# Neighbourhood attention on one core: keys in strips of eight columns with one value tile per row group, and nine of twelve second-stage units by seven products

## The chip, the cores and the metric

The kernel runs on one core of a Trainium2 chip. The metric is the device time of one execution in microseconds; the median of the runs is given. TensorE (PE) multiplies matrices, VectorE (DVE), ScalarE (ACT) and GpSimd (POOL) work element by element, and SyncE (SP) issues nearly all DMA transfers, in the order of its program.

## The reference, cut to what matters

One layer: an RMS norm, a projection of 2048 tokens of 1024 numbers onto queries, keys, values and a gate (4 x 1024 columns), neighbourhood attention on a grid of 32 rows by 64 columns with 16 heads of 64, a gate, an output projection, a residual and a final RMS norm.

```python
def reference(x, norm_0, w_in_0, rpb_0, w_out_0, norm_1, w_in_1, w_out_1, norm_f):
    h = rmsnorm(x, norm_0)
    q, k, v, gate = jnp.split(h @ w_in_0, 4, axis=-1)
    o = neighbourhood_attention(q, k, v, rpb_0)   # 16 heads of 64
    x = x + (o * jax.nn.silu(gate)) @ w_out_0
    return rmsnorm(x, norm_f)
```

Each token attends to 8 rows by 16 columns of keys around it, clipped at the grid's edges, with a bias that depends on the head and on the two offsets:

```python
rs = jnp.clip(r - kh // 2, 0, rows - kh)
...
s = jnp.where(col_valid[None, None], s + bias[None], NEG_INF)
p = jax.nn.softmax(s.reshape(B, H, nb, NA_QBLOCK, kh * NA_KBLOCK), axis=-1)
...
o = jnp.einsum('bhnqkj,bknjhd->bnqhd', p, vr)
```

## The kernel before

**Precision.** The projections split each float32 operand into a high and a low part and multiply three times (high by high, high by low, low by high). One tile of 128 by 512 results over 1024 inputs so costs 24 matmuls of 512 columns. Scores are done the same way; transposes and value products are float32.

**Stage one** (`stage_one`, line 546) works on the first 1024 tokens: all values, then the twelve units (kind, j) of k, q and g with j from 0 to 3, 256 columns each. A unit is a 2 by 2 block product, done by `seven_products` (line 378) in seven products of 12 matmuls, 84, where four plain tiles take 96. It costs sums and splits on DVE and ACT (`form`, `sum_`, `add`, `out_`, lines 390 to 431); `evac` and `give` (lines 309 and 321) evacuate results, split k into two parts, put q into query order, apply the gate's function, and store to DRAM.

**Stage two** (`stage_two`, line 756) does the second 1024 tokens: all values, and by seven products only the units of `units_two` (line 221). The remaining units stand in `halves` (line 222) and are done later in the plain way by `projections` and `group` (lines 868 and 346), 24 matmuls for each tile.

**The attention loop** (lines 1337 to 1356) has 64 turns and two more to drain. There are 32 pieces of work, the head pairs p = 0 to 7 by the row groups T = 0 to 3 of eight query rows (`order`, line 893), and each takes two turns, for column groups C = 0, 1 and then 2, 3 of 16 columns. So one tile of queries is 8 rows by 16 columns, 128 tokens. `KEY_ROWS` and `KEY_COLS` give the keys it can see: 11, 15, 15 or 12 rows by 24, 32, 32 or 24 columns.

In turn i the program emits, in this order: loads and biases (`begin`), matmuls from the filling (`feed`), the normalisation of turn i - 1, the transposes of turn i - 2 (`turns`), the scores of turn i, and the value products of turn i - 2 (`values`). Every engine works in program order. A score tile goes from PSUM through DVE, which adds the bias and takes the maximum (line 995), ACT's exponential with its sum (line 998), DVE's reciprocal (line 1004), POOL's scaling (line 1006), TensorE's transposes (line 1011), and copies to SBUF by DVE for the first half of the queries (line 1036) and by ACT for the second (line 1035, and the rest after it), to the value products (line 1056). POOL also makes the biases (`bias`, line 970): six sums whenever the head pair or the kind of row group changes.

**The filling.** `feed(n)` draws n matmuls from the projections that are left and then from the output projection (`outputs`), which needs all head pairs of a row group. `amount` (line 1272) says how many for each turn: 22 in each of the first 48 turns and 19.67 in the last 18. Up to 12 may be drawn ahead when an evacuation was just emitted (line 1280). The program's clock counts filling matmuls; stores and loads are put off by so many of them (`store`, `later_loads`, `due`), and `begin` emits all loads that are still put off.

**Values.** `evac_v` stores values to DRAM by head pair; `copy_v` (line 942), called throughout both stages, copies the 24 or 32 columns that each column group sees from DRAM to DRAM into `vc`, four rows interleaved on a partition index; `load_v` (line 932) loads one such tile for each piece and column group. `blocks` (line 61) cuts the keys of a row group into blocks of four rows: two that both halves of the queries (four rows each) see, and one or two that one half sees. The last block of row groups 0, 1 and 2 has three rows and so a copy of its own on ACT.

## Time and profile before

| | us |
|---|---|
| median of 3 runs | 1085.62 (1084.97 to 1085.65) |
| the profiled execution | 1086.36 |
| its span, first to last instruction | 1084.5 |

In the profile's lines a row names the line of the kernel, the engine, the operation, the tiles (out<-in), shapes and a count; after the bar come the busy time in us, the mean of one in ns, and the engine's idle time just before with what ended it. In the order of time a row begins with the start and the length in us. PE stands for TensorE's matmuls, PEld for its weight loads. The granted clock is that of TensorE as a share of full speed. Ends of matmuls are modelled, so counts of matmuls in a stretch are better than their busy time.

The seven products of stage one run from 96.6 to 325 us, the values of stage two to 414 us, its seven products to 471 us, the attention loop with its filling to about 1028 us, and the last output rows to the end.

### The profile page before, as it was taken

Reading aid. Unit: us, or ns where it says so; the run is one execution under the profiler, and the core shown is the slowest. Engines: PE = TensorE matmul, PEld = TensorE weight load, DVE = VectorE, ACT = ScalarE, POOL = GpSimd, SP = SyncE. Lnnn points to the kernel's source line nnn. Section 1 sums busy time; section 2 is a strip of 40 time slices with the busy share of each in tenths; the row PEclk is TensorE's granted clock in tenths of the full one; section 3 lists DMA queues with packets and bytes.
Section 4 is the critical chain, followed back from the end, with each engine's and each line's share of the span. In section 5 each row is a group of like instructions: output and inputs, shape, how many; then the busy total and the mean of one; then the engine's idle time right before and its main releaser. Section 6 shows DMA issues by size and latency. Waiting matters only on the chain.

```text
span 1084.5 us, 21929 instructions
## 1 busy us (share of the span) xinstructions
PE 1071.1 (99%) x7657; PEld 877.1 (81%) x7657; DVE 703.2 (65%) x1644; ACT 531.2 (49%) x1345; POOL 357.9 (33%) x474
## 2 busy tenths in 40 slices
PE   9999999999999999999999999999999999999997
PEld 6888888888888888887888888888888787888885
DVE  5376778778997535576555555664676786776643
ACT  7545334333434334346555555564576565665431
POOL 0000222312221000017545534444447656566200
PEclk9999999999999999999999999999999999999999
DMA  9633557574764366889868876886899787887442
GB/s 313 212 97 106 202 173 210 163 232 146 256 188 143 108 172 170 258 277 310 245 205 267 253 216 204 255 269 200 246 319 294 230 268 231 274 262 226 126 149 78
DMA packets 145901, 231.90 MB, mean 214 GB/s; under 512 B 13824, under 2 KB 61184, under 8 KB 145792
## 3 DMA queue, kind: packets, MB, share of 16 engines
q1 hardware_dynamic: 145648, 230.25, 68.2%
q8 instruction: 61, 1.00, 0.4%
q14 instruction: 48, 0.39, 0.1%
q10 hardware_dynamic: 144, 0.26, 0.1%
HBM read 171.73 MB, written 73.40 MB: 226 GB/s over the span
## 4 chain that ended last, share of the span: by engine, by line
PE 92%; DVE 3%; DMA 1%; ACT 1%; issue 1%; SPq 0%; POOL 0%; ACTq 0%; DVEq 0%; POOLq 0%
PE pp L411 23%; PE pv L531 16%; PE o L1056 8%; PE s L988 6%; PE pp L359 6%; PE pp L357 6%; PE pp L355 6%; PE po L1254 6%; PE po L1252 5%; PE po L1250 5%; PE ph L1011 5%; PE zp L1269 1%; DMA k_hi<-hi 1%; DMA land<-in_xt_dram 0%; DVE f L394 0%
## 5 line engine op out<-in xcount | busy, mean ns | idle before, releaser
L1006 POOL TENSOR_SCALAR x<-x,st 128x360 f32<-128x360 f32 (+5 forms) x256 | 143.0, 578 | 235.0 <-DVE st L1004 192.3
L970 POOL TENSOR_TENSOR em<-e,mk 128x480 f32<-128x480 f32 (+5 forms) x160 | 136.3, 886 | 138.3 <-DMA raw<-in_xt_dram 135.0
L998 ACT ACTIVATE x<-x,st 128x360 f32<-128x360 f32 (+5 forms) x256 | 151.8, 595 | 44.4 <-DVE st L995 44.4
L411 PE MATMUL pp<-h,f 128*128 128x512 f32 x480 | 155.4, 389 | 0.0
L430 POOL TENSOR_TENSOR tmp<-tmp,rb 128x512 f32<-128x512 f32 x36 | 58.9, 1637 | 270.6 <-DVE tmp L428 223.7
L411 PE MATMUL pp<-t,f 128*128 128x512 f32 x540 | 130.0, 390 | 0.3 <-DVE u L422 0.2
L995 DVE CUSTOM_DVE_ANT_0 x<-s,em 128x360 f32<-128x360 f32 (+5 forms) x256 | 124.0, 539 | 5.3 <-PE s L988 1.4
L411 PEld LDWEIGHTS pp<-t,f 128*128 128x128 f32 x540 | 101.2, 188 | 22.2 <-DVE u L422 1.2
L359 PE MATMUL pp<-h,w 128*128 128x512 f32 x288 | 115.1, 400 | 0.0
L357 PE MATMUL pp<-l,w 128*128 128x512 f32 x288 | 113.2, 393 | 0.0
L355 PE MATMUL pp<-h,w 128*128 128x512 f32 x288 | 113.1, 393 | 0.0
L1035 ACT ACTIVATE pta<-ph 96x256 f32<-96x256 f32 (+1 forms) x224 | 58.5, 333 | 104.3 <-PE ph L1011 104.3
L1036 DVE COPY pta<-ph 128x384 f32<-128x384 f32 (+3 forms) x128 | 60.7, 514 | 72.7 <-PE ph L1011 72.5
L411 PEld LDWEIGHTS pp<-h,f 128*128 128x128 f32 x480 | 90.1, 188 | 18.8
L1254 PE MATMUL po<-wol,gh 128*128 128x512 f32 x252 | 100.3, 398 | 0.0
L1252 PE MATMUL po<-woh,gl 128*128 128x512 f32 x252 | 98.9, 393 | 0.0
L1250 PE MATMUL po<-woh,gh 128*128 128x512 f32 x252 | 98.9, 392 | 0.0
L1056 PEld LDWEIGHTS o<-pta,vt 96*64 96x64 f32 (+2 forms) x1792 | 83.6, 137 | 17.2 <-issue 10.2
L1056 PE MATMUL o<-pta,vt 96*64 96x128 f32 (+4 forms) x1792 | 92.3, 254 | 1.4 <-DVE pta L1036 1.0
L411 PE MATMUL pp<-l,f 128*128 128x512 f32 x240 | 93.4, 389 | 0.0
L531 PE MATMUL pv<-wh,h 128*128 128x512 f32 x256 | 88.1, 390 | 0.0
L531 PE MATMUL pv<-wh,l 128*128 128x512 f32 x256 | 88.0, 389 | 0.0
(148 smaller groups left out, 1916.6 us busy)
## 6 DMA issues: line engine op xcount, KB each, us to landing
raw<-in_wg_dram SPq DMA_DIRECT2D x126, 256.0 KB, 5.1
e<-in_rpb_dram SPq DMA_DIRECT2D x54, 240.0 KB, 3.9
vt<-vc SPq DMA_DIRECT2D x64, 192.0 KB, 3.7
row<-in_xr_dram SPq DMA_DIRECT2D x32, 256.0 KB, 4.3
vd<-v SPq DMA_DIRECT2D x32, 256.0 KB, 3.0
k_hi<-hi SPq DMA_DIRECT2D x32, 256.0 KB, 2.6
k_lo<-lo SPq DMA_DIRECT2D x32, 256.0 KB, 3.8
vc<-vd SPq DMA_DIRECT2D x32, 256.0 KB, 4.4
```

The lines of the kernel that those rows point to most:

```text
L355: nc.tensor.matmul(p, wh[w, b][:, cols], hh[k, c], start=(k == 0), stop=False)
L357: nc.tensor.matmul(p, wh[w, b][:, cols], hl[k, c], start=False, stop=False)
L359: nc.tensor.matmul(p, wl[w, b][:, cols], hh[k, c], start=False, stop=(k == NK - 1))
L411: nc.tensor.matmul(B[n, P], t[:, int(m == 2), c], x[k][int(m == 1)], start=P in (1, 6, 5) and k == 0 and m == 0, stop=k == 3 and m == 2, s ...
L531: nc.tensor.matmul(ps[t], a[:, o], b, start=k == 0 and m == 0, stop=k == NK - 1 and m == 2)
L970: (nc.gpsimd if attending[0] or not s else nc.vector).tensor_tensor(sh(t), E[p, s][:, u0 + 4:u1 + 4, v0 + 8:v1 + 8], sh(MK[0][:, m0:m0 + n ...
L998: nc.scalar.activation(X[i, C][s], X[i, C][s], AF.Exp, bias=st[:, s:s + 1], scale=-1.0, accum_out=st[:, 2 + s:3 + s])
L1006: nc.gpsimd.tensor_scalar(X[i, C][s], X[i, C][s], st[:, 4 + s:5 + s], 0.5, op0=OP.mult, op1=OP.mult)
L1056: nc.tensor.matmul(o[s * 64:s * 64 + 64, C * 128 + q0:C * 128 + q0 + nq], vt[C][:k, g - g0_, s * 64:s * 64 + 64], t[:k, at:at + nq], start ...
L1250: nc.tensor.matmul(p, gh, woh[q, j], start=(i == 0), stop=False)
L1252: nc.tensor.matmul(p, gl, woh[q, j], start=False, stop=False)
L1254: nc.tensor.matmul(p, gh, wol[q, j], start=False, stop=(i == NK - 1))
```

## The change

The tokens of a grid row are put in the order (column within a strip, strip), with eight strips of eight columns; `x` for the norm's rows and the transposed `x` come to the chip in that order. Values are stored in token order, and one load per piece brings all eight strips: partition = (key row, column within the strip), 4 KB on each. Keys are put back into column order when they are split; queries, gate and output into the order (strip, row, column). The query tile is the same 8 by 16 tokens, with its halves now by columns, so `strips` takes the place of `blocks`: blocks are strips of eight columns by all 11, 15, 15 or 12 rows, 88, 120, 120 or 96 keys. Score tiles, masks and biases are laid out strip by strip. The copies `vc` from DRAM to DRAM go.

Apart from this, `units_two` has nine units in place of three, and the filling of the first 48 turns falls to 9.5 matmuls a turn, with 8 more in each of the first three; the amount that may be drawn ahead falls from 12 to half of a turn's amount.

```diff
-def blocks(T):
-    r0, r1 = KEY_ROWS[T]
+def strips(C):
     out = []
-    for g in range(r0 // 4, (r1 + 3) // 4):
-        halves = [h for h in range(2) if abs(2 * T + h - g) <= 1]
-        out.append((g, 4 * g - r0, min(4, r1 - 4 * g), halves[0] * 64, len(halves) * 64))
+    for s in range(KEY_COLS[C][0] // 8, KEY_COLS[C][1] // 8):
+        halves = [h for h in range(2) if abs(2 * C + h - s) <= 1]
+        out.append((s, s - KEY_COLS[C][0] // 8, halves[0] * 64, len(halves) * 64))
...
-    units_two = [(k, j) for j in range(1) for k in "kqg"]
-    halves = [(k, j, 1, c) for j in range(1, 4) for g in (("k", "q", "g") if j < 3 else ("k", "qg")) for c in (2, 3) for k in g]
+    units_two = [(k, j) for j in range(3) for k in "kqg"]
+    halves = [(k, j, 1, c) for j in range(3, 4) for g in ("k", "qg") for c in (2, 3) for k in g]
...
     def tiled(t):
-        return t.rearrange("p (r C c) -> p C r c", r=8, c=16)
+        return t.rearrange("p (r c s) -> p s r c", c=8, s=8)
 
     def blocked(t):
-        return t.rearrange("p (C r c) -> p C r c", r=8, c=16)
+        return t.rearrange("p (s r c) -> p s r c", r=8, c=8)
+
+    def by_place(t):
+        return t.rearrange("p (r c s) -> p r s c", c=8, s=8)
+
+    def by_column(t):
+        return t.rearrange("p (r s c) -> p r s c", s=8, c=8)
...
-        nc.scalar.activation(hi, t, AF.Copy)
-        nc.vector.tensor_tensor(lo, t, hi.bitcast(F32), OP.subtract)
+        nc.scalar.activation(by_column(hi), by_place(t), AF.Copy)
+        nc.vector.tensor_tensor(by_column(lo), by_place(t), by_column(hi.bitcast(F32)), OP.subtract)
...
-    def load_v(p, T, C):
+    def load_v(p, T):
         r0, r1 = KEY_ROWS[T]
-        g0_, g1_ = r0 // 4, (r1 + 3) // 4
-        c0, c1 = KEY_COLS[C]
-        def block():
-            VT[p, T, C] = t = vp([128, 4, 128], F32, "vt")
-            nc.sync.dma_start(t[:4 * (c1 - c0), :g1_ - g0_], vc[p, C][:, g0_:g1_])
-
-        return [block]
-
-    def copy_v(p, C, h):
-        must(*[("v", p // 4, t) for t in range(8 * h, 8 * h + 8)])
-        c0, c1 = KEY_COLS[C]
-        g = slice(512 * h, 512 * h + 512)
-        nc.sync.dma_start(vc[p, C].rearrange("(r c) g d -> c r (g d)", r=4)[:, :, g],
-                          vd[p // 4][p % 4].rearrange("r c g d -> c r (g d)")[c0:c1, :, g])
+        must(*[("v", p // 4, t) for t in range(r0 // 2, (r1 + 1) // 2)])
+        rows = vd[p // 4][p % 4].rearrange("(k s) d -> k s d", s=8)[8 * r0:8 * r1]
+        VT[p, T] = t = vp([128, 1024], F32, "vt").rearrange("p (s d) -> p s d", s=8)
+        nc.sync.dma_start(t[:8 * (r1 - r0)], rows)
...
-        sh = lambda a: a.rearrange("p (u v) -> p u v", v=v1 - v0)
+        sh = lambda a: a.rearrange("p (s u v) -> p s u v", u=u1 - u0, v=8)
...
-                sh(t), E[p, s][:, u0 + 4:u1 + 4, v0 + 8:v1 + 8], sh(MK[0][:, m0:m0 + n]), OP.add)
+                sh(t), E[p, s][:, u0 + 4:u1 + 4, v0 + 8:v1 + 8].rearrange("p u (s v) -> p s u v", v=8), sh(MK[0][:, m0:m0 + n]), OP.add)
...
-                    nc.tensor.matmul(pst[s], qq[a, qs], kk[a, :r1 - r0, c0:c1], start=(m == 0), stop=(m == 2))
+                    nc.tensor.matmul(pst[s], qq[a, qs], kk[a, :r1 - r0, c0:c1].rearrange("p r (s c) -> p s r c", c=8), start=(m == 0), stop=(m == 2))
...
             for h in range(2):
-                four = sum(b[2] == 4 for b in halves_[h])
-                k = 4 * width(C)
+                n = len(halves_[h])
                 put = (lambda o, i_: nc.scalar.activation(o, i_, AF.Copy)) if h else nc.vector.tensor_copy
-                put(slots[:k, h, :2 * four], ph[h][:k, :128 * four].rearrange("p (n q) -> p n q", q=64))
-                if four < len(halves_[h]):
-                    k = halves_[h][four][2] * width(C)
-                    put(slots[:k, h, 2 * four:2 * four + 2],
-                        ph[h][:k, 128 * four:128 * four + 128].rearrange("p (n q) -> p n q", q=64))
+                put(slots[:k, h, :2 * n], ph[h][:k, :128 * n].rearrange("p (n q) -> p n q", q=64))
...
     early = 96 * (12 - len(units_two)) + 192
-    amount = [early / 48] * 48 + [(384 - 30) / 18] * 18
+    first = 8
+    amount = [(early - 3 * first) / 48] * 48 + [(384 - 30) / 18] * 18
+    calm_debt = amount[0] / 2
+    for i in range(3):
+        amount[i] += first
...
-        while credit[0] > 0 or credit[0] > -12 and clock[0] - state["event"] < calm:
+        while credit[0] > 0 or credit[0] > -calm_debt and clock[0] - state["event"] < calm:
...
-        if 0 < i <= N:
-            p, T, cs = pairs[i - 1]
-            later_loads(load_v(p, T, cs[0]) + load_v(p, T, cs[1]), 0, 2)
+        if i % 2 == 0 and i < N:
+            load_v(*order[m])
```

More of the change, by code (lines that the diff above doesn't have):

```diff
@@ L1006, in normalise, with split @@
                 nc.gpsimd.tensor_scalar(X[i, C][s], X[i, C][s], st[:, 4 + s:5 + s], 0.5, op0=OP.mult, op1=OP.mult)
-    def turn(dst, i, C, s, blk, q0, nq):
-        g, lr, nr = blk[:3]
-        w = width(C)
-        nc.tensor.transpose(dst[:nr * w], X[i, C][s][q0:q0 + nq, lr * w:(lr + nr) * w],
-                            ident[q0:q0 + nq, q0:q0 + nq])
-    def split(T):
-        bl = blocks(T)
-        return [b for b in bl if b[4] == 128], [b for b in bl if b[4] == 64]
+    def split(C):
+        return [b for b in strips(C) if b[3] == 128], [b for b in strips(C) if b[3] == 64]
     def turns(i):
         p, T, cs = pairs[i]
-        full, part = split(T)
-        halves_ = [full + [b for b in part if b[3] == 64 * h] for h in range(2)]
+        k = 8 * (KEY_ROWS[T][1] - KEY_ROWS[T][0])
         for C in cs:
+            full, part = split(C)
+            halves_ = [full + [b for b in part if b[2] == 64 * h] for h in range(2)]
             t = PT[i, C] = pa([128, 768], F32, "pta")
```

69 lines of the change are left out of this document (32 added, 37 removed).

## The prediction

> **What bounds the kernel now.** I read the page first, then the table of stretches, then the order of time inside one turn of the attention loop.
>
> ```profile
> span 1084.5 us, 21929 instructions
> ...
> PE 1071.1 (99%) x7657; PEld 877.1 (81%) x7657; DVE 703.2 (65%) x1644; ACT 531.2 (49%) x1345; POOL 357.9 (33%) x474
> ...
> PE 92%; DVE 3%; DMA 1%; ACT 1%; issue 1%; SPq 0%; POOL 0%; ACTq 0%; DVEq 0%; POOLq 0%
> ```
>
> TensorE is busy for 99% of the span and carries 92% of the chain that ended last. Matmul ends are modelled, so busy time is not work; the work is read from counts per stretch. The next fence has the stretches of all engines (busy time and count of each engine, granted clock, DMA share, GB/s), and then the same stretches for line 995 alone, which runs eight times in a turn of the loop.
>
> ```profile
> core 0: us, PE busy (x) PEld busy (x) DVE busy (x) ACT busy (x) POOL busy (x), PEclk, DMA share, GB/s
> 300.00:400.00 100.00, 100.00 (x443) 82.77 (x442) 64.07 (x93) 37.66 (x68) 9.87 (x6) 1.00 0.53 153
> ...
> 499.40:614.90 115.50, 115.50 (x1084) 94.75 (x1078) 62.01 (x206) 64.33 (x202) 61.10 (x100) 1.00 0.80 251
> 614.90:784.60 169.70, 169.70 (x1734) 139.51 (x1733) 95.75 (x276) 94.38 (x276) 74.56 (x108) 1.00 0.75 233
> 784.60:889.20 104.60, 104.04 (x1075) 84.42 (x1072) 78.74 (x217) 66.76 (x194) 64.50 (x86) 1.00 0.88 278
> ...
> 499.40:614.90 115.50, 24.02 (x112) 1.00 0.80 251
> 614.90:784.60 169.70, 40.92 (x152) 1.00 0.75 233
> 784.60:889.20 104.60, 25.83 (x96) 1.00 0.88 278
> ```
>
> From 300 to 400 us, 443 matmuls of 512 columns ran in 100 us: 0.226 us each, at full granted clock. In the three attention stretches there are 112/8 = 14, 152/8 = 19 and 96/8 = 12 turns, so a turn lasts 8.25, 8.93 and 8.72 us. No other engine is near its limit now: the fullest are DVE with 78.74/104.60 = 75% in the third stretch and POOL with 62%.
>
> One turn in order of time, row group 0:
>
> ```profile
> 523.74 0.73 PE L1011 MATMUL ph<-ident,x 64*96 64x64 f32 x17
> 525.10 0.43 DVE L995 CUSTOM_DVE_ANT_0 x<-s,em 128x264 f32<-128x264 f32 x1
> 527.08 0.39 PE L355 MATMUL pp<-h,w 128*128 128x512 f32 x1
> 527.15 0.57 ACT L998 ACTIVATE x<-x,st 128x352 f32<-128x352 f32 x1
> 528.25 0.62 ACT L495 ACTIVATE qh<-qr 128x512 fp32r<-128x512 f32 x1
> 528.99 0.68 DVE L496 SCALAR_TENSOR_TENSOR ql<-qr,qh 128x512 fp32r<-128x512 f32 x1
> 531.18 0.39 PE L355 MATMUL pp<-h,w 128*128 128x512 f32 x1
> 531.78 0.22 DVE L1004 RECIPROCAL st<-st 128x2 f32<-128x2 f32 x2
> 531.95 0.74 PE L1011 MATMUL ph<-ident,x 64*128 64x64 f32 x17
> 532.13 2.03 POOL L1006 TENSOR_SCALAR x<-x,st 128x264 f32<-128x264 f32 x4 [9.66 <-DVE st L1004]
> 532.45 0.75 DVE L1036 COPY pta<-ph 128x256 f32<-128x256 f32 x2 [0.45 <-PE ph L1011]
> 534.11 4.71 POOL L970 TENSOR_TENSOR em<-e,mk 128x264 f32<-128x264 f32 x6
> ```
>
> The turn runs from transposes to transposes, 523.74 to 531.95. Line 355 is every third filling matmul; from 527.08 to 531.18 there are six triples, 18 matmuls in 4.10 us, 0.2278 each. A turn has 22 of them, 5.01 of its 8.21 us; 3.2 us are scores, transposes and value products. DVE and ACT finish in the shadow of the filling. So the filling is TensorE work and also the cover for everybody else's latency.
>
> **The change part by part.** *Matmuls.* Six units (k, q, g for j = 1 and 2) leave the loop's filling, where each takes 96 matmuls on the second half of the tokens, and join the second stage with seven products of 12, or 84. Removed: 576 x 0.2278 = 131.2 us. Added: 504 x 0.226 = 113.9 us. On TensorE this is -17.3 us. The counts of scores, transposes and value products are the same: column strips give 2 whole and 1 or 2 half blocks as row blocks did.
>
> *Thinner turns.* Filling falls from 22 to 9.5 per turn in the first 48 turns (17.5 in the first three). That is 12.5 x 0.2278 = 2.85 us less cover: by TensorE alone the three stretches go from 8.25, 8.93 and 8.72 to 5.40, 6.08 and 5.87 us a turn. What is late next is the loop that goes through DVE and ACT in their program order: line 995, exponentials, the filling's evacuations and splits, reciprocal, the copies of line 1036, line 995 again. In row group 0 it is 525.10 to 527.72 for line 995 and exponentials (2.62 us), 0.62 + 0.68 for splitting q in every other turn, 0.22, and 0.75: 4.9 us. The 9.5 fillings bring about 0.8 further ACT operations of 0.62 us, 0.5: 5.4 with the q split, 4.8 to 4.9 without it, against TensorE's 5.40. For 15 key rows the same rows are longer:
>
> ```profile
> 651.22 1.02 DVE L1036 COPY pta<-ph 128x384 f32<-128x384 f32 x2 [0.35 <-PE ph L1011]
> 652.39 0.66 DVE L995 CUSTOM_DVE_ANT_0 x<-s,em 128x480 f32<-128x480 f32 x1
> 655.04 0.58 ACT L998 ACTIVATE x<-x,st 128x360 f32<-128x360 f32 x1
> ```
>
> 652.39 to 655.62 is 3.23; with 1.30, 0.22, 1.02 and 0.5 the loop is 6.3 us with a q split and 5.7 without, against 6.08 and 5.87. I take waits of 0 in row group 0, 0.1 x 19 = 1.9 in the second stretch and, since the output evacuations fall there, 0.3 x 12 = 3.6 in the third: +5.5 us. The ends are 0 (all hidden, as now) and 0.5 in each of 45 turns, 22 us.
>
> *The first turns.* The pipeline starts behind a DVE backlog:
>
> ```profile
> 483.47 0.43 DVE L995 CUSTOM_DVE_ANT_0 x<-s,em 128x264 f32<-128x264 f32 x1
> 491.48 5.15 POOL L970 TENSOR_TENSOR em<-e,mk 128x264 f32<-128x264 f32 x6
> 496.62 2.02 POOL L1006 TENSOR_SCALAR x<-x,st 128x352 f32<-128x352 f32 x4
> 498.92 0.74 PE L1011 MATMUL ph<-ident,x 64*128 64x64 f32 x17
> ```
>
> The second pair's transposes (498.92) come 0.3 us behind its normalisation, which stands behind six bias sums, so this moment is set by POOL and DVE, not by filling. Up to it TensorE now has 4 x 22 = 88 fillings, then 3 x 17.5 + 9.5 = 62. The 26 missing ones, 5.9 us, are idle time if nothing else moves; with less filling in DVE's queue (one operation of 0.69 us) I take +5. Ends: 0 and 6.
>
> *Layout.* Keys in strips make the moving operand of the scores runs of 8 elements in place of 24 or 32. Mean times of such a matmul:
>
> ```profile
> L988 PE MATMUL s<-kt,qh 64*128 64x360 f32 x128 | 18.0, 346 | 0.0
> L988 PE MATMUL s<-kt,qh 64*128 64x352 f32 x64 | 11.1, 350 | 0.9 <-DVE lo L342 0.9
> ```
>
> 15 runs of 24 take no longer than 11 runs of 32, so I take 0. The upper end is 1 ns for each further run, about 33 x 6 pairs x 64 turns = 13 us. Tokens ordered with the strip innermost make q's evacuations, k's splits and the gate product read every eighth element. No row shows that. The nearest contiguous rows and the fullest DVE stretch (the last three units of the first stage):
>
> ```profile
> L428 DVE TENSOR_TENSOR tmp<-pp,u 128x512 f32<-128x512 f32 x30 | 20.6, 688 | 19.8 <-PE pp L411 19.3 <-issue 0.5
> L342 DVE TENSOR_TENSOR lo<-tmp,hi 128x512 fp32r<-128x512 f32 x19 | 12.9, 681 | 3.2 <-ACT hi L341 3.2
> ...
> sum 57.21, PE 57.00 PEld 46.86 DVE 54.20 ACT 23.12 POOL 15.31; mean PE 19.00 PEld 15.62 DVE 18.07 ACT 7.71 POOL 5.10
> ```
>
> At no extra cost the price is 0; at twice the time, 8 operations more of 0.69 us in those units make DVE 59.7 of 57.2 us: 2.5 us. Elsewhere DVE has room. I take +1. The Trainium skill, page "SBUF — State Buffer" (section on the port formula, its note on cachelines), speaks against this edit: a line is 16 bytes, and full rate wants two accesses in each; a step of 32 bytes gets one. By it the term would be the 2.5 us end, and nothing else in the sum would move; no row here can show it.
>
> *Copies and loads.* The 64 copies of values from DRAM to DRAM go, and one load of 4 KB rows takes the place of four. On the chain that ended last DMA has 1%, so this is 0, at DMA shares of 0.75 to 0.88. Of ACT's copies of transposes 96 (three row groups, 32 each) merge into their neighbours:
>
> ```profile
> L1035 ACT ACTIVATE pta<-ph 96x128 f32<-96x128 f32 x48 | 13.0, 271 | 0.0
> ```
>
> The two forms of 48 take 26 us in 48 turns, 0.54 a turn; about half returns as wider copies. It is off the loop above, where line 1036 is as long: 0, at best 0.1 us a turn.
>
> **Sum.** Against the profiled execution's own time, 1086.36 us (span 1084.5 and 1.9 around it): -17.3 + 5.5 + 5 + 1 = -5.8, 1080.6. The median of the runs stands 0.74 lower: 1079.8, so **1080**.
>
> **Rivals.** *All is covered.* The waits are 0, the start costs 0: 1085.6 - 17.3 = 1068.3. For it: slack of all engines in the table. Against: the start rows. Chance 0.2.
>
> *The loop eats it.* Waits of 0.25 us in each of 45 turns in place of 5.5 in all, and the start: -17.3 + 11.3 + 5 + 1 = 0: 1085.6, no change. For it: the loop of 6.3 us against 6.08. Chance 0.17.
>
> *POOL becomes the bound*, slower. It does 61.10/14 = 4.36 us a turn in the first stretch and 64.50/12 = 5.4 (about 5.2 with thinner filling) in the third, against TensorE's 5.40 and 5.87. In these every other turn has six bias sums, which now read the bias table in runs of 8. If each takes x longer, POOL adds 3x a turn. It decides from x = 0.35 us in the first and 0.22 in the third, on 0.79 us (4.71/6). At double time, x = 0.79: 4.36 + 2.37 - 5.40 = 1.3 us x 14, and 5.2 + 2.37 - 5.87 = 1.7 x 12, or 39 us in all: about 1080 + 39 - 4 (its loop waits are in it) = 1115; at x = 0.5 it is 0.5 x 14 + 0.8 x 12 = 16 us, 1093. Against: it idles 9.66 us ahead of the normalisation at 532.13, and that wait is for DVE. Chance 0.15.
>
> *Late loads*, slower too. Delays are counted in filling matmuls. The gate tile is asked for with a delay of 15, more than a turn now holds.
>
> ```profile
> 522.07 0.44 SPq L952 DMA_DIRECT2D sgt<-sgd  x1
> 535.16 0.69 DVE L1070 TENSOR_TENSOR og<-o,sgt 128x512 f32<-128x512 f32 x1
> sgt<-sgd SPq DMA_DIRECT2D x32, 256.0 KB, 6.5
> ```
>
> Now it has 13.1 us for 6.5. It will be issued by the start of the next turn, 5.4 us before its use, or about 6.4 as SP runs ahead. The product of line 1070 then holds up DVE's queue, and with it line 1036 and the value products: 24 row groups x 0.7 us = 17 us, 1097. It decides when landing exceeds that lead by more than DVE's idle time. Chance 0.1.
>
> **Numbers.** Forecast 0.38, all covered 0.2, no change 0.17, POOL 0.15, late loads 0.1. Faster than 0.2% (2.2 us, about what a measurement tells from no change) is 0.58, within it 0.17, slower 0.25. The likeliest case's own range is 1074 to 1083; the range for 8 in 10 goes from all covered, 1068, to the lower prices of the slow cases, 1096.
>
> **What would show it.** Right: second stage longer by 114 us; turns of 5.4 to 6.2 us up to the 48th; idle time of TensorE before lines 988 and 1056 released by line 1036; a gap of some 5 us in the first four turns; bias sums still near 0.8 us each. Wrong: bias sums over 1.1 us with transposes waiting for POOL; line 1070 waiting for the gate tile; score matmuls above 350 ns at 352 columns; DVE's strided operations at 0.69 (the term of 1 falls) or 1.4 us with gaps in the first stage.

## The result, and the profile after

The change made the kernel **slower**: 1104.19 us (median of 4 runs, 1102.15 to 1104.89) against 1085.63, a ratio of 1.0167 with a 95% interval of 1.015 to 1.0185, or 18.6 us. The forecast was 1080, and the range ended at 1096. The profiled execution took 1104.89 us; its span and the busy times, from the page of the changed kernel:

```profile
span 1103.1 us, 21471 instructions
...
PE 1076.3 (98%) x7585; PEld 872.4 (79%) x7585; DVE 788.7 (71%) x1716; ACT 547.5 (50%) x1267; POOL 364.3 (33%) x474
...
PE 56%; DVE 5%; ACT 4%; POOL 3%; issue 2%; DMA 1%; SPq 0%; DVEq 0%; POOLq 0%; ACTq 0%
```

PE is still the engine that is "busy" nearly all the time. Two lines give the loss away. DVE went from 703.2 to 788.7 us. Part of this is work that the change adds: the six units bring 72 more operations (1644 before, 1716 now), and with the units alone (E2 below) DVE has 744.6 us. The rest goes with the layout: with its strided reads repaired (E3 below) DVE has 749.0. The other line is the chain that ended last. Its shares now sum to 71%, since it could be followed back only to 311.5 us of the span. PE has 56 of them, and even if all of the rest were PE's it would have 85%, where it had 92% before. So DVE, ACT and POOL have come onto the path.

The table of stretches of the changed kernel (columns as before), cut at its stages: start, stage-one products, stage-two values, stage-two products, turns 0 to 3, 4 to 14, 15 to 35, 36 to about 48, the rest.

```profile
97.30:334.30 237.00, 232.49 (x1011) 189.93 (x1010) 207.85 (x281) 97.40 (x171) 63.54 (x35) 0.99 0.50 156
...
422.00:597.50 175.50, 175.50 (x775) 145.08 (x773) 115.27 (x170) 61.88 (x101) 2.86 (x4) 1.00 0.46 147
597.50:629.50 32.00, 29.39 (x230) 22.60 (x230) 21.09 (x61) 18.13 (x50) 15.00 (x24) 0.84 0.79 260
629.50:690.90 61.40, 60.93 (x789) 49.70 (x785) 43.04 (x151) 41.05 (x124) 43.88 (x75) 1.00 0.82 258
690.90:823.70 132.80, 128.99 (x1509) 101.61 (x1505) 105.79 (x302) 92.81 (x253) 83.75 (x119) 1.00 0.83 259
823.70:905.90 82.20, 77.52 (x876) 61.63 (x872) 68.28 (x201) 52.15 (x143) 67.98 (x90) 0.98 0.82 257
```

Two things are to be seen. The column of the granted clock has 0.84 in the first four turns, 0.98 late in the loop and 0.99 in stage one, where before every stretch ahead of the tail had 1.00. And PE idles 4.5 us of the 237.0 in stage one, a stretch in which the prediction saw a loss of 1 us. The same stretch of the kernel before, for comparison:

```profile
96.60:326.30 229.70, 229.35 (x1011) 189.26 (x1010) 190.51 (x281) 88.70 (x171) 57.02 (x35) 1.00 0.62 193
```

With the same 281 operations DVE is busy 207.85 us in place of 190.51.

The next table tells the 18.6 us by stretch. Turns begin at their first score matmul; "by counts" is the change in filling matmuls times 0.2278, or the added 504 times 0.226; "lost" is what the two kernels' difference leaves over. The last two columns are the losses of two experiments told below, each half of the change.

| stretch | before | after | by counts | lost | predicted loss | layout alone (E1) | units alone (E2) |
|---|---|---|---|---|---|---|---|
| start | 96.6 | 97.3 | 0 | 0.7 | 0 | -0.7 | -0.6 |
| stage one, products | 229.7 | 237.0 | 0 | 7.3 | 1 | 5.4 | 0 |
| stage two, values | 87.8 | 87.8 | 0 | 0 | 0 | 0 | 0 |
| stage two, products | 56.9 | 171.1 | +113.9 | 0.3 | 0 | 0 | 0.3 |
| to the first scores | 7.6 | 4.4 | -3.2 | 0 | 0 | 0 | 0 |
| turns 0 to 3 | 29.2 | 31.9 | -4.6 | 7.3 | 5 | -0.1 | 6.1 |
| turns 4 to 14 | 90.9 | 61.4 | -32.3 | 2.8 | 0 | 1.4 | 1.9 |
| turns 15 to 35 | 186.0 | 132.8 | -62.0 | 8.8 | 1.9 | 0.5 | 7.7 |
| turns 36 to 46 | 98.8 | 75.0 | -30.5 | 6.7 | 3.6 | -0.2 | 6.7 |
| turns 47 to 62 | 127.2 | 130.3 | +1.4 | 1.7 | 0 | 2.7 | 0 |
| tail | 73.9 | 74.1 | 0 | 0.2 | 0 | 0.1 | -0.2 |
| sum | 1084.5 | 1103.1 | -17.3 | 35.8 | 11.5 | 9.1 | 21.9 |

The counts moved as forecast, and at the prices of the prediction they are worth its 17.3 us. The losses are three times what was forecast.

**Stage one.** The record of the granted clock has a stretch at half rate from 185.0 us, 3.41 us long. The matmuls of the products in order of time, just ahead of it (start, length, and the idle time before with its releaser):

```profile
181.68 0.39 PE L422 MATMUL pp<-h,f 128*128 128x512 f32 x1
183.88 4.54 PE L422 MATMUL pp<-t,f 128*128 128x512 f32 x12 [1.81 <-DVE u L433]
```

TensorE waits 1.81 us for a sum on DVE (line 433, the `add` of `seven_products`), and then twelve matmuls take 4.54 us, where twelve at full clock take 2.7. On DVE two of the splits of line 353 stand ahead of that sum:

```profile
175.74 2.18 DVE L353 TENSOR_TENSOR lo<-tmp,hi 128x512 fp32r<-128x512 f32 x1
...
180.90 1.12 DVE L353 TENSOR_TENSOR lo<-tmp,hi 128x512 fp32r<-128x512 f32 x1
...
183.15 0.67 DVE L433 TENSOR_TENSOR u<-pp,p 128x512 f32<-128x512 f32 x1
```

There are four such waits; these are the first rows of the table of PE's waits in the changed kernel (total us, times, longest):

```profile
PE ph L1014 <- POOL x L995: 4.6, 9, 1.7
PE pp L422 <- DVE u L433: 4.4, 4, 1.8
PE s L977 <- DVE pta L1018: 3.8, 6, 2.1
```

What made DVE late stands in the table of groups, shapes kept apart. All nine rows are 128 by 512 elements. Lines 352 and 353 (k's split) read every eighth element, of `tmp` in SBUF or of `pp` in PSUM; line 326 (q) reads `rb` in that way from SBUF, where its neighbour 324 reads both operands in order; 1048 reads the gate tile so. Of 439 and 441 a third, the q units, read `u` and `rb` so.

```profile
L352 ACT ACTIVATE hi<-tmp 128x512 fp32r<-128x512 f32 x25 | 30.1, 1204 | 44.4 <-POOL tmp L441 27.2 <-DVE tmp L439 14.1 <-DVE tmp L324 2.0
L352 ACT ACTIVATE hi<-pp 128x512 fp32r<-128x512 f32 x7 | 4.1, 584 | 1.2 <-PE pp L370 1.1
...
L1048 DVE TENSOR_TENSOR og<-o,sgt 128x512 f32<-128x512 f32 x32 | 38.3, 1198 | 6.2 <-DMA sgt<-sgd 3.9 <-PE o L1032 2.0
L439 DVE TENSOR_TENSOR tmp<-pp,u 128x512 f32<-128x512 f32 x42 | 35.3, 841 | 21.4 <-PE pp L422 21.3
...
L353 DVE TENSOR_TENSOR lo<-tmp,hi 128x512 fp32r<-128x512 f32 x25 | 31.6, 1264 | 9.0 <-ACT hi L352 8.2
...
L324 DVE TENSOR_TENSOR tmp<-pp,rb 128x512 f32<-128x512 f32 x8 | 5.5, 689 | 3.7 <-PE pp L422 3.7
L353 DVE TENSOR_TENSOR lo<-pp,hi 128x512 fp32r<-128x512 f32 x7 | 4.8, 683 | 0.7 <-ACT hi L352 0.7
...
L326 DVE TENSOR_TENSOR tmp<-pp,rb 128x512 f32<-128x512 f32 x4 | 4.6, 1141 | 0.0
...
L441 POOL TENSOR_TENSOR tmp<-tmp,rb 128x512 f32<-128x512 f32 x36 | 65.4, 1822 | 272.0 <-DVE tmp L439 202.8 <-issue 29.0 <-ACT row L193 27.7
```

The stride costs 0.5 to 0.6 us on DVE and 0.6 on ACT when it is read from SBUF (683 to 1264, 689 to 1141, 584 to 1204 ns). Where a third of the operations read so, the means went from 688 to 841 ns (line 439, 428 before) and on POOL from 1637 to 1822. When every eighth element is read from PSUM it costs nothing that shows: 683 ns on DVE here, and 681 to 689 in order.

**The first turns.** TensorE in order of time, around the transposes of the first pair:

```profile
608.64 0.39 PE L368 MATMUL pp<-l,w 128*128 128x512 f32 x1
610.71 0.26 PE L1014 MATMUL ph<-ident,x 64*88 64x64 f32 x2 [1.69 <-POOL x L995]
611.17 0.87 PE L1014 MATMUL ph<-ident,x 64*88 64x64 f32 x10 [0.21 <-POOL x L995]
...
619.01 0.63 PE L366 MATMUL pp<-h,w 128*128 128x512 f32 x1
619.44 0.63 PE L368 MATMUL pp<-l,w 128*128 128x512 f32 x1
619.86 0.63 PE L370 MATMUL pp<-h,w 128*128 128x512 f32 x1
```

The transposes wait 1.69 us for POOL's scaling, which was foreseen. What was not: from 611.7 us on the clock's record shows half rate for 10.24 us, and eight us after the wait the filling's matmuls still start 0.42 to 0.43 us apart in place of 0.2278. The idle time itself is small. In the table of stretches above TensorE idles 32.00 - 29.39 = 2.6 us in these four turns, and in the same turns of the kernel before 29.20 - 27.97 = 1.2:

```profile
478.50:507.70 29.20, 27.97 (x232) 22.35 (x232) 20.26 (x63) 19.15 (x56) 15.40 (x24) 1.00 0.82 259
```

So 1.4 us of the 7.3 lost are more idle time, and up to half of 10.24, 5.1, go with the clock.

**Inside thin turns.** DVE and PE in a turn of row group 1, cut to the rows that matter:

```profile
745.55 1.17 DVE L1048 TENSOR_TENSOR og<-o,sgt 128x512 f32<-128x512 f32 x1 [1.61 <-DMA sgt<-sgd]
...
746.62 1.08 DVE L184 TENSOR_TENSOR wol<-raw,woh 128x512 fp32r<-128x512 f32 x1
...
747.62 0.67 DVE L340 SCALAR_TENSOR_TENSOR sg<-sg,pp 128x512 f32<-128x512 f32 x1
748.22 0.21 DVE L993 RECIPROCAL st<-st 128x2 f32<-128x2 f32 x2
...
748.35 0.75 PE L977 MATMUL s<-kt,qh 64*128 64x480 f32 x4 [0.76 <-DVE sg L340]
748.35 0.86 DVE L1018 COPY pta<-ph 120x256 f32<-120x256 f32 x2
```

The gate product waits 1.61 us for its gate tile and then takes 1.17 us; behind it in DVE's order stand a split, the gate, the reciprocal and the copy of the transposes. TensorE's scores stand 0.76 us, until line 340, the gate, is done. All PSUM tiles of the kernel come from one pool of eight (lines 109 and 112), and line 340 reads one of them. So the scores, not only the value products, come behind DVE's queue.

### The profile page after: what moved, and what is told of

It reads as the page before. It is cut to its first block, busy times and chain, and to the rows that moved or that the text cites. A ratio compares the mean times of both kernels' runs of the same rounds, so it can differ in the third digit from the quotient of the medians.

```text
span 1103.1 us, 21471 instructions
## 1 busy us (share of the span) xinstructions
PE 1076.3 (98%) x7585; PEld 872.4 (79%) x7585; DVE 788.7 (71%) x1716; ACT 547.5 (50%) x1267; POOL 364.3 (33%) x474
## 4 chain that ended last, share of the span: by engine, by line
PE 56%; DVE 5%; ACT 4%; POOL 3%; issue 2%; DMA 1%; SPq 0%; DVEq 0%; POOLq 0%; ACTq 0%
PE pp L422 16%; PE pv L542 8%; PE o L1032 6%; PE s L977 5%; PE po L1232 5%; PE po L1228 4%; PE po L1230 4%; PE ph L1014 3%; ACT x L987 2%; PE pp L370 2%; PE pp L366 1%; POOL x L995 1%; PE pp L368 1%; POOL em L959 1%; DMA ograw<-ogd 1%
## 5 line engine op out<-in xcount | busy, mean ns | idle before, releaser
L422 PE MATMUL pp<-h,f 128*128 128x512 f32 x672 | 217.6, 389 | 0.0
L422 PE MATMUL pp<-t,f 128*128 128x512 f32 x756 | 184.0, 393 | 4.4 <-DVE u L433 4.4
L422 PEld LDWEIGHTS pp<-t,f 128*128 128x128 f32 x756 | 142.2, 189 | 36.6 <-DVE u L433 7.0
L1032 PEld LDWEIGHTS o<-pta,vt 120*64 120x64 f32 (+2 forms) x1792 | 85.8, 140 | 19.1 <-issue 15.1
L977 PE MATMUL s<-kt,qh 64*128 64x480 f32 (+5 forms) x512 | 90.5, 385 | 6.5 <-DVE pta L1018 3.8
L1032 PE MATMUL o<-pta,vt 120*64 120x128 f32 (+5 forms) x1792 | 94.6, 258 | 0.5 <-ACT pta L1017 0.3
L405 DVE TENSOR_TENSOR f<-raw,f 128x512 fp32r<-128x512 f32 x105 | 78.3, 746 | 20.9 <-ACT f L404 20.9
L542 PE MATMUL pv<-wl,h 128*128 128x512 f32 x256 | 87.9, 389 | 0.0
L1017 ACT ACTIVATE pta<-ph 120x384 f32<-120x384 f32 (+5 forms) x128 | 52.4, 458 | 68.3 <-PE ph L1014 68.2
L1018 DVE COPY pta<-ph 120x384 f32<-120x384 f32 (+5 forms) x128 | 62.5, 514 | 31.5 <-PE ph L1014 31.2
```

The lines of the kernel that those rows point to most:

```text
L405: nc.vector.tensor_tensor(t[:, 1], src, t[:, 0].bitcast(F32), OP.subtract)
L422: nc.tensor.matmul(B[n, P], t[:, int(m == 2), c], x[k][int(m == 1)], start=P in (1, 6, 5) and k == 0 and m == 0, stop=k == 3 and m == 2, s ...
L542: nc.tensor.matmul(ps[t], a[:, o], b, start=k == 0 and m == 0, stop=k == NK - 1 and m == 2)
L977: nc.tensor.matmul(pst[s], qq[a, qs], kk[a, :r1 - r0, c0:c1].rearrange("p r (s c) -> p s r c", c=8), start=(m == 0), stop=(m == 2))
L1032: nc.tensor.matmul(o[s * 64:s * 64 + 64, C * 128 + q0:C * 128 + q0 + nq], vt[:k, strip, s * 64:s * 64 + 64], t[:k, at:at + nq], start=firs ...
```

## The experiments

Ratios are to the kernel before in runs on the same chip.

| | us, median | ratio (95%) |
|---|---|---|
| the change | 1104.19 | 1.0167 (1.015 to 1.0185) |
| E1 layout alone | 1096.06 | 1.0099 (1.008 to 1.0118) |
| E2 units and thin turns alone | 1092.71 | 1.0057 (1.0042 to 1.0072) |
| E3 change, reordered on PSUM reads | 1097.33 | 1.0105 (1.0088 to 1.0122) |
| E4 change, 14 more fillings in first turns | 1105.63 | 1.0181 (1.0148 to 1.0213) |
| E5 layout before, 6 units | 1081.72 | 0.9968 (0.9957 to 0.9979) |
| E6 E2, transposes earlier | 1118.87 | 1.0316 (1.0292 to 1.0341) |
| E7 E2, last x splits later | 1093.68 | 1.0079 (1.0062 to 1.0096) |
| E8 E3, keys read in rows | 1096.04 | 1.0097 (1.0081 to 1.0112) |
| E9 E1, reordered on PSUM reads | 1092.45 | 1.0064 (1.0052 to 1.0076) |
| E10 E9, keys read in rows | 1085.74 | 1.0000 (0.9992 to 1.0009) |
| E11 E10, 6 units | 1084.59 | 0.9987 (0.9978 to 0.9997) |
| E12 layout before, 7 units | 1083.97 | 0.9978 (0.9969 to 0.9988) |

### The two halves: E1 and E2

E1 is the changed kernel with the units, the filling and the drawing ahead of before:

```diff
-    units_two = [(k, j) for j in range(3) for k in "kqg"]
-    halves = [(k, j, 1, c) for j in range(3, 4) for g in ("k", "qg") for c in (2, 3) for k in g]
+    units_two = [(k, j) for j in range(1) for k in "kqg"]
+    halves = [(k, j, 1, c) for j in range(1, 4) for g in (("k", "q", "g") if j < 3 else ("k", "qg")) for c in (2, 3) for k in g]
...
-    first = 8
+    first = 0
...
-    calm_debt = amount[0] / 2
+    calm_debt = 12
```

> The change with its layout and its value tiles, but three second-stage units and 22 fillings a turn as before. Theory (reads of every eighth SBUF element cost DVE and ACT time that shows where TensorE has no cover, above all in the first stage; thick turns hide the rest): first stage 7 us longer, attention loop within 2 us of before, about 1093 us. Rival (the whole loss is from thin turns, the layout costs nothing): 1085.6 us within 2.

E2 is the kernel before with the nine units, the filling and the drawing ahead of the change (the diff of E1 the other way, in the old layout).

> The kernel before with nine second-stage units, 9.5 fillings a turn and 8 more in the first three, and nothing of the layout. Theory (the thin turns and the thin start lose by themselves: start 8 to 10 us, turns 10 to 17 us, against 17 us won): 1087 to 1096 us, no gap in the first stage. Rival (the layout makes the loss, thin turns are covered): 1069 to 1075 us.

Measured: 1096.06 and 1092.71, so +0.99% and +0.57%, together 1.56% against the 1.67% of the change. The halves add up nearly, and each of them alone is a loss. Their stretches are in the table above: E1 loses in stage one (5.4 us, where 7 were expected) and in the loop (4.3 us, more than the 2 expected); E2 loses nothing before the loop and 22 us in its first 47 turns, more than the 17.3 that the counts bring. In these profiled executions the halves lose 31.0 us together and the change 35.8; what is over stands in the start (2.0), in stage one (1.9, where the change has its stretch at half clock) and in the first turns (1.3).

### The reads: E3 and E9

The reordering of k, q, g and gate moved to operations that read PSUM, or that read and write runs of 8; what is computed is the same, and the only operations more are copies on ACT of gate tiles of the second half, 7 in E3 (1274 operations against 1267) and 13 in E9 (1262 against 1249). Its core (E3 against the changed kernel, E9 against E1):

```diff
-        if kind != "q":
-            nc.vector.tensor_tensor(tmp, p, rb[c], OP.mult)
+        lay, of, with_ = laid(kind)
+        nc.vector.tensor_tensor(lay(tmp), of(p), with_(rb[c]), OP.mult)
...
-        nc.scalar.activation(by_column(hi), by_place(t), AF.Copy)
-        nc.vector.tensor_tensor(by_column(lo), by_place(t), by_column(hi.bitcast(F32)), OP.subtract)
+        of = by_place if psum else by_column
+        nc.scalar.activation(by_column(hi), of(t), AF.Copy)
+        nc.vector.tensor_tensor(by_column(lo), of(t), by_column(hi.bitcast(F32)), OP.subtract)
...
-            nc.vector.tensor_tensor(blocked(og), blocked(o), tiled(SG.pop((p, T))), OP.mult)
+            nc.vector.tensor_tensor(blocked(og), blocked(o), runs(SG.pop((p, T))), OP.mult)
```

> The change, but every reordering of tokens is done while reading PSUM or in runs of eight contiguous elements, so that no DVE, ACT or POOL instruction reads every eighth element of SBUF; the only operations more are copies of PSUM for the few gate tiles of the second half. Theory: DVE's k and q operations go from 1.13 and more to 0.69 us and ACT's from 1.21 to 0.63; the first stage loses its gaps and its half-clock stretch, 7 us; the gate product of the loop goes from 1.2 to 0.7 us and gives 1 to 4 us: 1093 to 1097 us. Rival (first-stage gaps come from load order or POOL): 1102 to 1105 us.

> The strips with the filling and the units of before, and with every reordering done on a read from PSUM or on runs of eight. The strips alone had cost 10.4 us (1096.1 against 1085.6), 5.4 of them in the products of stage one. Theory (the reads of every eighth element from SBUF made those 5.4 us, and some DVE and ACT time in the loop): the products of stage one take 229.7 us again and the time is 1089 to 1092, what is left being score matmuls with their moving operand in runs of 8. Rival (the strips cost by their longer copies and by their loads, and stage one only moved what waits later): 1094 to 1097.

Measured: 1097.33 and 1092.45, each less than 0.5 us above its theory's range. In both the products of stage one take 229.7 us again. That stretch in E3, and rows with the operations that were slow:

```profile
96.20:325.90 229.70, 229.36 (x1011) 189.25 (x1010) 190.56 (x281) 88.84 (x171) 56.95 (x35) 1.00 0.51 161
...
L1062 DVE TENSOR_TENSOR og<-o,sgt 128x512 f32<-128x512 f32 x32 | 22.1, 689 | 8.7 <-DMA sgt<-sgd 4.9 <-PE o L1046 3.2 <-issue 0.5
L365 DVE TENSOR_TENSOR lo<-tmp,hi 128x512 fp32r<-128x512 f32 x25 | 17.1, 683 | 7.1 <-ACT hi L364 7.0
...
L364 ACT ACTIVATE hi<-tmp 128x512 fp32r<-128x512 f32 x25 | 15.8, 630 | 46.4 <-POOL tmp L455 27.3 <-DVE tmp L453 15.4 <-DVE tmp L333 2.0
```

All are back at the contiguous price, with the reordering still done, and DVE is busy 190.56 us again for its 281 operations. So the strided reads from SBUF are shown to be the cause of the loss in stage one, 7.3 us of the change. In E3 the loop did not get faster (turns 0 to 62 took 401.5 us in both): DVE's 0.5 us on each gate product and split is not what the thin turns wait for.

### The scores' moving operand: E8 and E10

The score matmuls read the keys row by row (runs of 24 or 32) and write their PSUM tile in runs of 8, in place of the other way round:

```diff
-                    nc.tensor.matmul(pst[s], qq[a, qs], kk[a, :r1 - r0, c0:c1].rearrange("p r (s c) -> p s r c", c=8), start=(m == 0), stop=(m == 2))
+                    nc.tensor.matmul(pst[s].rearrange("p (s r c) -> p r s c", r=r1 - r0, c=8), qq[a, qs],
+                                     kk[a, :r1 - r0, c0:c1].rearrange("p r (s c) -> p r s c", c=8), start=(m == 0), stop=(m == 2))
```

> The change with reordering from PSUM (1097.3 us), and the score matmuls read keys in runs of 24 or 32 as before and write PSUM in runs of 8. Theory (the moving operand in runs of 8 costs 0.6 ns a run: pairs of 480 columns 253 ns apart in place of 224): pairs again 224 ns apart, 0.1 us a turn, 4 to 7 us less: 1090 to 1093 us. Rival (runs of 8 cost as much where they are written): 1097 us.

> As the run before, and the score matmuls read the keys in runs of 24 or 32 and write PSUM in runs of 8. Theory (these two access patterns are the whole price of the strips): 1084 to 1087, pairs of scores at 120, 131, 165 and 177 us/1000 apart as before the change. Rival (something else in the layout costs too: half of the transposes' copies are longer, or one load of 4 KB rows collides with others): 3 us or more above the kernel before, 1088.5 to 1092, with the score pairs at the old distances all the same.

The 64 by 480 score matmul in the group tables of the kernel before, of the change and of E10, in this order:

```profile
L988 PE MATMUL s<-kt,qh 64*128 64x480 f32 x128 | 22.9, 414 | 0.4 <-ACT pta L1035 0.4
```

```profile
L977 PE MATMUL s<-kt,qh 64*128 64x480 f32 x128 | 28.3, 439 | 4.0 <-DVE pta L1018 2.4 <-DVE sg L340 0.8 <-DVE y L1139 0.5
```

```profile
L991 PE MATMUL s<-kt,qh 64*128 64x480 f32 x128 | 25.1, 405 | 1.4 <-DVE pta L1033 1.4
```

439 ns against 414 and 405. The starts say it better than these lengths, whose ends are modelled. Median time from the third to the fifth start of a tile's six matmuls, one pair of matmuls:

| elements | further runs of 8 | before | E9 (runs of 8) | E10 (rows) |
|---|---|---|---|---|
| 264 | 22 | 120 ns | 135 | 119 |
| 288 | 24 | 129 | 148 | 131 |
| 352 | 33 | 164.5 | 179 | 164.5 |
| 360 | 30 | 164 | 181 | 165 |
| 384 | 36 | 178.5 | 205.5 | 176 |
| 480 | 45 | 224 | 253 | 225 |

A further run costs 0.44 to 0.79 ns, mean 0.64. Weighted by the tiles a pair is 21 ns longer, and 6 pairs x 64 turns x 21 ns = 8.0 us. Against this, E10 is 6.7 us faster than E9 in thick turns. In E1 the loop as a whole lost only 4.3 us, so a part of the 8.0 comes back elsewhere in the loop; where is not shown. E10 takes 1085.74, within 0.1% of the kernel before: **the two access patterns are the whole price of the strips** where turns are thick. In thin turns (E8 against E3) the repair brings 0.9 us only by the ratios, less than the spread of these runs, and its theory's 1090 to 1093 was missed. E8's profiled execution has 13.7 us at half clock ahead of the tail, E3's 6.8, so other waits take its place there.

### The first turns: E4 and E7

E4, against the change: `first = 14` in place of 8, so more filling in turns 0 to 2.

> The change with 14 in place of 8 further fillings in each of the first three turns (23 a turn there, 9.1 after). Theory (the start waits for the normalisation of the first two pairs, 2.6 us idle, and this idle time brings 10 us at half clock, 5 us): no stretch of half clock at the start, the start 6 to 8 us shorter, the later turns 1.2 us longer together: 1097 to 1099 us. Rival (the wait is only moved, the half clock comes from the transposes and scores, not from idle time): 1103 to 1105 us.

Measured: 1105.63 (1101.79 to 1109.95). Turns 0 to 3 took 28.9 us in place of 31.9, but the scores of the first turn came 2.3 us later, half clock was still there (615.4 us, 6.8 long) and two further stretches of 3.4 us came at 775.8 and 840.7, in turns that had become thinner. The wait was moved, not removed.

E7, against E2: the filling of the last quarter in another order, so that the splits of its x come later in DVE's queue.

```diff
-    halves = [(k, j, 1, c) for j in range(3, 4) for g in ("k", "qg") for c in (2, 3) for k in g]
+    halves = [(k, j, 1, c) for j in range(3, 4) for g in ("kq", "g") for c in (2, 3) for k in g]
```

> Nine units without the layout, but the loop's filling takes k and q for the third quarter of the tokens before any for the fourth, so that the four inputs that DVE and ACT normalise and split at the head of the loop come later. Theory (the start waits behind these splits in DVE's queue: scores of turn 0 done at 590.1, line 995 ended at 596.6): no half clock at the start and the start 5 to 8 us shorter: 1085 to 1088 us. Rival (the start is bound by POOL's bias sums): 1091 to 1093 us.

Measured: 1093.68 against 1092.71 of E2. The profiled execution (1089.88, the fastest of four) has turns 0 to 3 at 26.5 us in place of 30.8, 1.1 of this by five filling matmuls that fall into later turns, and half the time at half clock at the start, but turns 4 to 14 at 62.5 in place of 60.4 and a stretch at half clock at 866.0. In that execution DVE's backlog was part of the start's wait; taking it away gained nothing in the median, and by the ratios, 1.0079 against 1.0057, it lost.

### Thin turns: E5, E12, E6

E5 is the kernel before with six units (15.5 fillings a turn), E12 with seven (13.5), each with the change's rules for filling. E12 against E5:

```diff
-    units_two = [(k, j) for j in range(2) for k in "kqg"]
-    halves = [(k, j, 1, c) for j in range(2, 4) for g in (("k", "q", "g") if j < 3 else ("k", "qg")) for c in (2, 3) for k in g]
+    units_two = [(k, j) for j in range(2) for k in "kqg"] + [("k", 2)]
+    halves = [(k, j, 1, c) for j in range(2, 4) for g in (("q", "g") if j < 3 else ("k", "qg")) for c in (2, 3) for k in g]
```

> The kernel before with six second-stage units, 15.5 fillings a turn and 8 more in the first three; nothing of the layout. Theory (the thin turns lose because the filling becomes shorter than the work of DVE and ACT in the loop, so the loss sets in late): 36 matmuls less, -8.6 us, start and turns lose 1 to 4 together: 1078 to 1082 us. Rival (each filling matmul taken out of a turn loses the same, half of what nine units lost): 1089 us.

> Layout of before, seven second-stage units by seven products (k for j = 2 joins the six), 13.5 fillings a turn. TensorE alone gains 2.9 us over six units (96 x 0.2278 - 84 x 0.226): 1078.8 if nothing waits. Nine units lose 11 us against six (1092.7 against 1081.7). Theory (the loss sets in gradually below 15 fillings, because the scores wait for the transposes' copies): 1080 to 1083, with 1 to 4 us of waits of scores for copies. Rival (the loss comes in steps, through idle time of about 2 us at the start of the loop that brings half clock): 1079 without a stretch at half clock, 1083 to 1086 with one, in the profile near 570 to 580 us.

Measured: 1081.72 and 1083.97. E5 is faster than both kernels, and within its theory's range. Time of a turn beyond its fillings (each 0.2278 us), in us:

| turns | 22 a turn (before) | 15.5 (E5) | 13.5 (E12) | 9.5 (E2) |
|---|---|---|---|---|
| 0 to 3 | 2.81 | 2.82 | 2.97 | 4.33 |
| 4 to 14 | 3.25 | 3.28 | 3.39 | 3.42 |
| 15 to 35 | 3.75 | 3.79 | 3.96 | 4.11 |
| 36 to 46 | 3.95 | 4.17 | 4.24 | 4.56 |

Summed over these 47 turns, 3.8 us are lost at 15.5 fillings, 9.9 at 13.5 and 22.4 at 9.5, against gains by counts of 8.7, 11.5 and 17.3. At 15.5 the loss is small, and 2.4 us of it fall in turns 36 to 46. From there it goes up turn by turn, as E12's theory has it; its time is 1 us above the theory's range, for TensorE's 2.9 us were more than eaten. Its rival fell, since 1084 came without half clock before the tail. The start breaks off only at 9.5. The largest waits of PE in E12 and, behind it, in E2:

```profile
PE o L1056 <- DVE pta L1036: 3.6, 4, 1.9
PE zp L1269 <- POOL z L1266: 1.9, 1, 1.9
PE ph L1011 <- POOL x L1006: 1.3, 5, 0.4
PE s L988 <- DVE pta L1036: 0.8, 2, 0.5
```

```profile
PE ph L1011 <- POOL x L1006: 3.7, 6, 1.8
PE s L988 <- DVE y L1161: 2.2, 3, 1.1
PE o L1056 <- DVE pta L1036: 2.2, 3, 1.7
PE s L988 <- ACT pta L1035: 2.1, 5, 1.1
PE zp L1269 <- POOL z L1266: 1.9, 1, 1.9
PE s L988 <- DVE pta L1036: 1.2, 4, 0.3
```

Scores and value products wait for the copies of transposes, and transposes for POOL. In E12 it is mostly the value products (3.6 us against 0.8), where its theory had the scores. Between score matmuls a turn of 15 to 35 spends 1.08 us before, 1.12 in E5, 1.18 in E12, 1.38 in E2 and 1.45 in the change (sums of the distances of starts), so 0.30 of the 0.36 us that E2 loses in such a turn stand between the scores. Transfers do not explain the loss: the DMA share in turns 4 to 46 is 0.94 to 0.96 in E2 and 0.82 to 0.83 in the change, and both lose about the same. E6 asks whether an earlier place of the transposes mends that. Against E2:

```diff
         middle(i)
+        if i > 1:
+            turns(i - 2)
         feed(a * 0.55, 8)
...
-        if i > 1:
-            turns(i - 2)
```

> Nine units without the layout (1092.7 us), but the transposes of turn i - 2 stand ahead of the last 55% of the filling of turn i, so that DVE's and ACT's copies of them run under that filling. Theory (scores and value products wait for these copies, which hold PSUM banks and stand in DVE's queue behind reciprocals and splits): time between scores from 1.38 back to some 1.1 us a turn in turns 15 to 47, 8 to 12 us less in all: 1081 to 1085 us. Rival (TensorE waits for the normalisation on POOL, which is then needed earlier): 1093 us or more.

Measured: 1118.87. The scores' part went back to 1.12 us, as the theory has it; the total went up by 28 us by the ratios, as its rival has it. PE's waits in E6:

```profile
PE ph L1011 <- POOL x L1006: 19.4, 38, 4.8
```

Transposes that come some five filling matmuls earlier wait for POOL's scaling 38 times, 19.4 us, and six stretches at half clock follow, one of them the tail's. Of the two places tried in a turn of 9.5 fillings, neither is both behind the normalisation and ahead of the scores' needs.

### Both repairs with six units: E11

E10 with E5's units, and with the filling that goes with them:

```diff
-    units_two = [(k, j) for j in range(1) for k in "kqg"]
+    units_two = [(k, j) for j in range(2) for k in "kqg"]
...
```

> Strips with both access patterns repaired, and six second-stage units by seven products (15.5 fillings a turn). The layout before with six units took 1081.7. Theory (the repaired strips cost nothing and the loss of thin turns sets in below some 15 fillings): 1081 to 1083. If the fewer copies and loads of the strips bring something where turns are thinner: 1077 to 1080. Rival (the strips have a further price which shows only in thinner turns): 1085 or more, with waits of the transposes for POOL or of the scores for the copies over 3 us in all.

Measured: 1084.59 (1081.40 to 1086.76), by the ratios 2.1 us above E5, with runs spread over 5 us. The spread goes with the granted clock: the two shortest, 1081.4 and 1081.6, had 0.998 over the span, as E5 has, and the others 0.993 to 0.996. The profiled execution (1086.64) has a stretch of 6.8 us at half clock at 797.4, and PE's waits:

```profile
PE s L991 <- DVE pta L1033: 3.5, 5, 1.5
PE s L991 <- DVE y L1154: 2.0, 1, 2.0
```

The theory's 1081 to 1083 was met by these two runs of twelve; the rival's conditions (waits for copies of over 3 us) are there, its 1085 is near the median. So the repaired strips have a small price in thinner turns, and it comes with time at a lower clock. That fewer copies and loads bring something did not show.

## Why the prediction was wrong, point by point

*Matmuls, -17.3.* Right: stage two's products took 114.2 us more, 113.9 foreseen, and the loop lost the counted 576 matmuls.

*Layout, +1 for every eighth element.* Wrong in size: 7.3 us in stage one. The step "at twice the time, 8 operations more of 0.69 us in those units make DVE 59.7 of 57.2 us: 2.5 us" had the double time right (0.68 to 1.26 us), and then looked at the sum of one stretch: DVE need not be full for TensorE to wait. It was 207.85 of 237.0 us busy, 88%, and the products still waited four times for the sum of line 433, because that sum stands behind the slow operations in DVE's order. On top, 3.4 us at half clock cost 1.7. E1 had the waits without that stretch, 5.4 us; E3 took both away. By the rule of the Trainium skill, page "SBUF — State Buffer" (section on the port formula, its note on cachelines), one access in each 16-byte line is below full rate, and the trace agrees: 1.26 against 0.68 us. The same note of the Trainium skill says as well that a pattern in PSUM which isn't contiguous slows matmuls significantly; score matmuls that write PSUM in runs of 8 in E10 did not slow (225 against 224 ns), so the measurement decides.

*Layout, 0 for the scores' runs of 8.* Wrong in size: 0.64 ns for each further run, 8.0 us by the distances and 6.7 by E9 against E10. The step "15 runs of 24 take no longer than 11 runs of 32, so I take 0" compared forms that differ by 4 runs, or 2.6 ns, in lengths with modelled ends that scatter by more. The upper end, 1 ns and 13 us, came nearer, but no row stood behind its 1 ns; it was kept for the range and left out of the sum. These prices are for thick turns; in the change's own thin turns E8 got back 0.9 us.

*The first turns, +5.* The place and the wait were right: the transposes wait for POOL's scaling. The price was not. What failed is "the 26 missing ones, 5.9 us, are idle time if nothing else moves": idle time grew by 1.4 us only, and the wait was followed by half clock, for 10.24 us in the change and 6.8 in E2, which the sum did not have. At half rate 10.24 us lose up to 5.1. That +5 stands near the 7.3 lost is luck. Over the whole span the stretches at half clock before the tail, 3.41 + 10.24 + 3.41 us, lose up to 8.5 us; the kernel before had none.

*Thinner turns, +5.5.* This is the largest error: 16.3 us in turns 4 to 46 in E2, 18.3 in the change. The step that failed is the comparison "the loop is 6.3 us with a q split and 5.7 without, against 6.08 and 5.87", from which 0.1 and 0.3 us a turn were taken. It sets a mean loop against a mean turn. But the loop's last piece, the copies, has a time inside the turn by which it is due, and the waits name two users for it: the value products, and ahead of them the scores (copies in lines 1035 and 1036, after the change 1017 and 1018). A gate product, an output's evacuation or a split in DVE's queue then stops TensorE even where the sums fit. That the scores wait because the copies, gates and evacuations set PSUM tiles free is argued from the rows and from the one pool of eight that all tiles share, and no run tests it; E6 shows only that earlier transposes mend the scores' part and pay for it with POOL. It is not the whole account either: in turns 4 to 46 of E2 the waits on record sum to 7.9 us of the 16.3 lost, 3.6 of them for the copies, and what holds the rest stays open. "Waits of 0.25 us in each of 45 turns" was a rival's price; E2 has 0.36 in turns 15 to 35 and 0.61 in 36 to 46.

*Copies and loads, 0.* Right: E10 shows no gain and no loss in the total.

*Rivals.* "POOL becomes the bound" is false: its sums of the bias over the six shapes took 878 ns on average, 886 before. "Late loads" is true in its mechanism and small: 3.9 us of DVE waiting in the whole run for the gate tile. "The loop eats it" named the right place and got half of the price. The slower outcome came from no single rival: four terms were each too small (the thin turns most, then the scores' runs, stage one and the first turns), while the range's upper end was taken from one rival at a time.

## What to carry to other kernels

Reorder on the read from PSUM, where every eighth element came free here, or in runs of 8, and never by a strided read from SBUF; keep a matmul's moving operand in long runs and put the permutation into its PSUM write. When filling is taken out of a software pipeline, the other engines' loop must fit ahead of the first consumer in the next turn, so go in steps: six units gained 3.5 us, seven 2, nine lost 6.5. And when TensorE is at the bound, price a wait of about 2 us with the time at half clock that may follow it.

## What the hardware showed that was not expected

- **Short waits were followed by half clock.** A wait of 1.69 us with three more of 0.2 to 0.4 among small transposes was followed by 10.24 us at half the granted clock; one of 1.81 us in stage one by 3.41 us. All such stretches ahead of the tails were 3.41, 6.83 or 10.24 us long, one to three times 3.41. All six waits of TensorE of 2.0 us and more in the products and loops of these runs had one begin within them or up to 2 us behind. Of the shorter ones some had and some had not: 1.66 us in E7 (at 864.5 us) did, 1.68 in E2 (at 865.7) and 1.93 in E12 (at 772.2) did not. What decides between them is not shown. The Trainium skill, page "TensorE: Matmul & The Clock Gate" (section on what is actually happening), has the clock fall after an idle window of about 3.4 us; here it also fell behind waits half as long.
- **The same stride, two prices.** Every eighth float of 128 by 512: 1.20 us on ACT and 1.26 on DVE from SBUF, 0.58 and 0.68 from PSUM. In order from SBUF it was 0.63 and 0.68 (E3).
- **Runs of 8 on a matmul:** 0.64 ns for each further run when read as the moving operand, none that shows when written to PSUM (E10).
